# A linear recurrence inside a gemm stream: level exponentials begun two levels ahead, key transposes later in two heads

## The chip, the cores and the metric

The kernel runs on one core of one Trainium2 chip. The metric is the device time of one execution in microseconds (us). Five engines work side by side: TensorE (PE in the profile; its weight loads are PEld), VectorE (DVE), ScalarE (ACT), GpSimd (POOL) and SyncE (SP), which here issues the loads of the weights. Each engine takes its instructions in a fixed order, and waits at an instruction until what that needs is there.

## The reference, cut to what matters

One layer of a hybrid network for 256 latent tokens and 256 context tokens, model width 2048. A joint input projection feeds two mixers: a differential attention, and a gated linear recurrence with 8 heads of 128 x 128, run in both directions. Their results are projected, gated, added and projected again; a gated MLP with a convolution follows. The change is in the recurrence:

```python
def rec_gate(f_raw, lower):
    f = lower + (1.0 - lower) * jax.nn.sigmoid(f_raw.astype(jnp.float32))
    return to_rec_heads(1.0 - f), to_rec_heads(jnp.log(f))

    def step(state, inp):
        kc, vc, gc = inp[0], inp[1], inp[2]
        b = jnp.cumsum(gc, axis=2)
        b_end = b[:, :, -1:, :]
        new_state = (jnp.exp(b_end)[:, :, 0, :, None] * state
                     + jnp.einsum('bhsk,bhsv->bhkv', kc * jnp.exp(b_end - b), vc))
        ...
        rel = jnp.exp(jnp.where(mask, b[:, :, :, None, :] - b[:, :, None, :, :], -jnp.inf))
        scores = jnp.einsum('bhtk,bhtsk,bhsk->bhts', qc, rel, kc)
        out = (jnp.einsum('bhts,bhsv->bhtv', scores, vc)
               + jnp.einsum('bhtk,bhkv->bhtv', qc * jnp.exp(b), state))
```

The score of token t for token s is a product over 128 features of q_t, k_s and the exponential of the difference of two running sums of log gates.

## The kernel before

**Gemms.** Weights come as f32 blocks of 128 x 1024 (`stage`, L65): a load into `raw`, a cast on ACT into `whi` (L72), the rest on DVE into `wlo` (L73). A projection tile takes two such blocks, called units here. A tile over latent and context tokens takes three matmuls for each 128 rows (L77 to L79, `acc<-h,whi` and `acc<-h,wlo`, 24 in a unit); one over latent tokens alone takes two (L136, L137, 16 in a unit). In the recurrence stage each head h needs four tiles: the two gates RFF and RFB and the values RI, of three matmuls, and the queries RQ, of two. The last RG tiles, of the output's gate, close the stage.

**Gates of a head.** After RFF, RFB and RQ the raw values lie in `fq`. `fold` brings RQ out of PSUM (L152 on ACT, L153 on DVE), then come a copy (L669), the sigmoid (L670), the query's product (L671), the scaling with the lower bound (L674), two lines on POOL that give k (`kkq`, L676, and `kc`, L677), two clampings (L678, L679), Ln (L680), a sum (L681), and five scans, the running sums: three into `PL` (L683), two into `PC` (L685). `PL` and `PC` have two buffers each, used in turn by the heads.

**A head's products.** `head` (L558 on) is a generator that puts down the rest of a head, and is interrupted by `yield n`. It computes `KQ` (exponentials of `PC` and `PL`, L561 to L564, and a product on DVE, L565, and on POOL, L568), transposes the values (`tp`, L597) and the scaled keys (`ktp`, L604), forms `dc` (L610 to L613: level 7 and the diagonal) and the states (`stp`, L620). The scores between the two halves of blocks of 2, 4, 8 ... 128 tokens are the levels 0 to 6. For each a factor tile `E` is made by `level(li)`: two subtractions (L586, L587), one exponential on ACT (L588), two products (L590, L591). The subtractions of levels 3 and 5 and the products of levels 2 and 4 are on POOL, all others on DVE. Four matmuls (`lv`, L629) multiply E's halves into PSUM, and DVE copies the result under a mask into the scores (`S4`, L632). At the end stands the output `op` (L637 to L640).

**What sets the order.** `tick(n)` is called after each unit of a gemm, with 2 for a three-matmul unit and 1 for another, and lets the first head in the list go on once its yields have run down; one head is served at a time, and the next one after it. So the yields set where in the gemm stream PE meets a head's products. A scheduler then orders the instructions of each engine by what depends on what and by a high priority for `stage`. `lv` has three PSUM buffers, the tag `ar` of the factors 16, `whi` and `wlo` three, `raw` four.

Of the kernel before, what the change touches and what calls it, by code (L numbers as in the profile page):

```python
# [41 lines left out]
def body(ctx, tc, cst_d, sel_d, cb_d, ccol_d, wn_d, xT_d, xc_d, lam_d, rope_d, mask_d, wm_d, wg0_d, win_d, wba_d,  # L42
# [325 lines left out]
    with ExitStack() as esa:  # L368
# [19 lines left out]
        with ExitStack() as es:  # L388
# [100 lines left out]
            for h in range(8):  # L489
                bg_rate[0] = BG_ATT0 if h < 2 else BG_ATT  # L490
                ks = in_tile(AK + h)
                kf = at.tile([P, 512], F32, tag="kf", name="kf")
                act.copy(kf[:, 256:], ks[:, 256:])
                kr = at.tile([P, T], F32, tag="qkr", name="kr", bufs=2)
                act.copy(kr, ks[:, :256])
                rope_apply(kf[:, :256], kr)
                kT = at.tile([P, 2, 512], F32R, tag="kT", name="kT", bufs=2)
                act.copy(kT[:, 0], kf)
                dve.tensor_sub(kT[:, 1], kf, kT[:, 0].bitcast(F32))

                vs = in_tile(AV + h)
                if AV + h in g0raw:
                    vr = vs
                else:
                    vr = big.tile([P, 512], F32, tag="ar", name="vr", bufs=16)
                    act.copy(vr, vs)

                qs = in_tile(AQ + h)
                qr = at.tile([P, T], F32, tag="qkr", name="qr", bufs=2)
                fold(qr, qs)  # L510
                rope_apply(qr, qr)
                qT = at.tile([P, 2, T], F32R, tag="qT", name="qT", bufs=2)
                act.copy(qT[:, 0], qr)
                dve.tensor_sub(qT[:, 1], qr, qT[:, 0].bitcast(F32))
                start(head(h, kT, vr, qT))
# [11 lines left out]
        with ExitStack() as es:  # L527
# [29 lines left out]
            def head(h, kkq, kc, PL, PC, vr):  # L557
# [16 lines left out]
                def level(li):  # L574
                    c = LEVELS[li]
                    shp = [P, 2, T // (2 * c), c]
                    Lv = AL.rearrange("p (d n w c) -> p d n w c", d=2, w=2, c=c)[:, :, :, 0]
                    Rv = AR.rearrange("p d (n w c) -> p d n w c", w=2, c=c)[:, :, :, 1]
                    rl = PL[:, 1:3, 0:T].rearrange("p d (n w) -> p d n w", w=2 * c)[:, :, :, c:c + 1].broadcast_to(shp)
                    rr = PL[:, 0:2, 0:T].rearrange("p d (n w) -> p d n w", w=2 * c)[:, :, :, c:c + 1].broadcast_to(shp)  # L580
                    E = big.tile([P, 2, T], F32, tag="ar", name="E", bufs=16)
                    Ev = E.rearrange("p d (n w c) -> p d n w c", w=2, c=c)
                    Lm = kkq[:, 0::2].rearrange("p d (n w c) -> p d n w c", w=2, c=c)[:, :, :, 0]
                    Rm = kkq[:, 1:3].rearrange("p d (n w c) -> p d n w c", w=2, c=c)[:, :, :, 1]
                    eng = pool if li in (3, 5) else dve
                    eng.tensor_tensor(Ev[:, :, :, 0], rl, Lv, ALU.subtract)  # L586
                    eng.tensor_tensor(Ev[:, :, :, 1], Rv, rr, ALU.subtract)  # L587
                    act.activation(E, E, AF.Exp)  # L588
                    eng = pool if li in (2, 4) else dve
                    eng.tensor_tensor(Ev[:, :, :, 0], Ev[:, :, :, 0], Lm, ALU.mult)  # L590
                    eng.tensor_tensor(Ev[:, :, :, 1], Ev[:, :, :, 1], Rm, ALU.mult)  # L591
                    return E

# [4 lines left out]
                vn = rt.tile([P, 4, P], F32, tag="vn", name="vn", bufs=2)  # L598
                act.copy(vn, tp)
                E7 = level(7)  # L600
                yield 2 if h in (0, 1, 7) else 1
                kt_ = rps.tile([P, 4, P], F32, tag="aux", name="ktp", bufs=2)
                for i in range(4):
                    pe.transpose(kt_[:, i], KQ[:, 0, i // 2, (i % 2) * P:(i % 2 + 1) * P], ident)  # L604
                kn = big.tile([P, 4, P], F32, tag="ar", name="kn", bufs=16)
                act.copy(kn, kt_)
                E = level(0)
                yield 1
                dc = rps.tile([P, 4, P], F32, tag="aux", name="dc", bufs=2)
                pe.matmul(dc[:, 1], E7[:, 0, 0:P], E7[:, 1, P:], start=True, stop=True)  # L610
# [10 lines left out]
                stn = rt.tile([P, 2, P], F32, tag="stn", name="stn", bufs=2)  # L621
                act.copy(stn, sp[:, 0:2])

                for li in range(7):
                    En = level(li + 1) if li < 6 else None
                    yield 1
                    lvp = rps.tile([P, 2, P], F32, tag="lv", name="lv", bufs=3)
                    for m in range(2):
                        pe.matmul(lvp[:, m], E[:, 0, m * P:(m + 1) * P], E[:, 1, m * P:(m + 1) * P],  # L629
                                  start=True, stop=True)  # L630
                    for m in range(2):
                        dve.copy_predicated(out=S4[:, 3 * m], mask=masks[:, li].bitcast(U32), data=lvp[:, m])  # L632
                    E = En
                yield 2
                op = rps.tile([P, 4, P], F32, tag="aux", name="op", bufs=2)
                o2 = op[:, 0:2].rearrange("p a b -> p (a b)")
# [20 lines left out]
            for h in range(8):  # L657
# [31 lines left out]
                else:  # L689
                    vr = big.tile([P, 512], F32, tag="ar", name="vr", bufs=16)  # L690
                    act.copy(vr, ri)
                start(head(h, kkq, kc, PL, PC, vr))
                if h == 0:

# [318 lines left out]
```

## Time and profile before

| | |
|---|---|
| median of three runs | 1888.81 us (1885.11 to 1890.86) |
| the profiled execution's own time | 1883.4 us |
| its span | 1881.6 us |
| PE busy | 1833.5 us, 97% |
| DVE busy | 1353.2 us, 72% |
| ACT busy | 997.2 us, 53% |
| POOL busy | 382.1 us, 20% |
| mean granted clock of TensorE | 0.995 |

The span is the time from the first to the last instruction of the profiled execution. Busy times are of the whole program; the recurrence stage lies from about 410 to 810 us. The rows further down say, for each line, when an engine began, how long it worked and, in brackets, how long it stood idle before and what ended that. Matmuls overlap their neighbours, so the distance of their starts says what one takes of PE's time, not their duration.

### The profile page before, as it was taken

How to read it: one execution, taken by the hardware profiler on the slowest of the kernel's cores; microseconds unless marked ns; L12 is line 12 of the kernel's file. 1: busy time of each engine (PE TensorE's matmuls, PEld its weight loads, DVE VectorE, ACT ScalarE, POOL GpSimd, SP SyncE). 2: the span in 40 equal slices, each digit the busy share in tenths (PEclk: the TensorE clock that was granted, in tenths of full speed). 3: DMA queues.
4: the chain of work that ended last, by engine and by line, in shares of the span. 5: the costliest groups of instructions: out<-in, count | busy, mean ns of one | idle time of the engine just before them, and what ended most of it. 6: DMA issues, size and time to landing. Idle time of an engine off the chain costs nothing.

```text
span 1881.6 us, 27926 instructions
## 1 busy us (share of the span) xinstructions
PE 1833.5 (97%) x10416; PEld 1558.2 (83%) x10416; DVE 1353.2 (72%) x2131; ACT 997.2 (53%) x1507; POOL 382.1 (20%) x328
## 2 busy tenths in 40 slices
PE   7999999999999999999999999999999999999997
PEld 4777777887788888888888889888888888888886
DVE  4449989779866667988886779776777677654444
ACT  4336444557655556744455557555555555534342
POOL 0002111103223333411111111222222222211111
PEclk9999999999999999999999999999999999999998
DMA  9977777474233333688997665666656666666664
GB/s 387 369 266 256 229 230 238 142 239 137 93 113 112 102 103 122 211 302 305 321 321 249 190 191 179 192 190 190 191 190 191 190 191 190 182 194 187 193 188 132
DMA packets 108711, 385.69 MB, mean 205 GB/s; under 512 B 12320, under 2 KB 12448, under 8 KB 108576
## 3 DMA queue, kind: packets, MB, share of 16 engines
q1 hardware_dynamic: 108576, 383.92, 63.1%
q8 instruction: 81, 1.33, 0.3%
q14 instruction: 54, 0.44, 0.1%
HBM read 381.78 MB, written 2.10 MB: 204 GB/s over the span
## 4 chain that ended last, share of the span: by engine, by line
PE 78%; DVE 11%; DMA 6%; issue 3%; ACT 2%; POOL 0%; SPq 0%; DVEq 0%; ACTq 0%; POOLq 0%
PE macc L136 30%; PE macc L137 15%; PE acc L136 6%; DMA bgraw<-in_wm 5%; PE acc L77 5%; PE acc L79 5%; PE acc L78 5%; DVE wlo L73 3%; PE acc L137 3%; PE g L187 2%; DVE bgraw L93 2%; PE acc L187 2%; PE nat L187 2%; PE lv L629 1%; ACT whi L72 1%
## 5 line engine op out<-in xcount | busy, mean ns | idle before, releaser
L73 DVE TENSOR_TENSOR wlo<-raw,whi 128x1024 fp32r<-128x1024 f32 (+1 forms) x514 | 628.6, 1224 | 240.0 <-ACT whi L72 234.7
L72 ACT CAST whi<-raw 128x1024 fp32r<-128x1024 f32 (+1 forms) x514 | 530.9, 1034 | 422.1 <-PE macc L136 159.2
L136 PE MATMUL macc<-h,whi 128*128 128x512 f32 x1344 | 466.0, 391 | 0.0
L137 PE MATMUL macc<-h,wlo 128*128 128x256 f32 x1344 | 376.3, 280 | 0.0
L136 PE MATMUL acc<-h,whi 128*128 128x512 f32 x896 | 320.9, 400 | 0.0
L136 PEld LDWEIGHTS macc<-h,whi 128*128 128x128 f32 x1344 | 251.3, 187 | 55.1
L137 PEld LDWEIGHTS macc<-h,wlo 128*128 128x128 f32 x1344 | 254.0, 189 | 0.0
L137 PE MATMUL acc<-h,wlo 128*128 128x256 f32 x896 | 252.5, 282 | 1.2 <-DVE wlo L73 1.0
L136 PE MATMUL macc<-f,whi 128*128 128x512 f32 x704 | 244.1, 391 | 0.0
L77 PE MATMUL acc<-h,whi 128*128 128x512 f32 x528 | 212.1, 402 | 0.0
L79 PE MATMUL acc<-h,wlo 128*128 128x512 f32 x528 | 207.3, 393 | 0.3 <-DVE wlo L73 0.3
L78 PE MATMUL acc<-h,whi 128*128 128x512 f32 x528 | 206.4, 391 | 0.0
L136 PEld LDWEIGHTS acc<-h,whi 128*128 128x128 f32 x896 | 168.4, 188 | 37.7 <-issue 0.4
L137 PE MATMUL macc<-f,wlo 128*128 128x256 f32 x704 | 197.1, 280 | 0.0
L137 PEld LDWEIGHTS acc<-h,wlo 128*128 128x128 f32 x896 | 169.3, 189 | 4.9 <-DVE wlo L73 4.3
L93 DVE SCALAR_TENSOR_TENSOR bgraw<-bgraw,cb 128x1024 f32<-128x1024 f32 x105 | 133.0, 1268 | 36.8 <-DMA bgraw<-in_wm 36.0
L136 PEld LDWEIGHTS macc<-f,whi 128*128 128x128 f32 x704 | 131.6, 187 | 28.9
L884 POOL TENSOR_TENSOR u<-u 128x256 f32<-128x256 f32 x44 | 69.2, 1572 | 326.5 <-DVE u L879 286.5
L137 PEld LDWEIGHTS macc<-f,wlo 128*128 128x128 f32 x704 | 133.1, 189 | 0.0
L77 PEld LDWEIGHTS acc<-h,whi 128*128 128x128 f32 x528 | 99.2, 188 | 22.8 <-issue 4.3
L79 PEld LDWEIGHTS acc<-h,wlo 128*128 128x128 f32 x528 | 99.1, 188 | 22.6 <-DVE wlo L73 0.8
L78 PEld LDWEIGHTS acc<-h,whi 128*128 128x128 f32 x528 | 99.3, 188 | 19.2 <-issue 0.4
(752 smaller groups left out, 2674.4 us busy)
## 6 DMA issues: line engine op xcount, KB each, us to landing
raw<-in_win SPq DMA_DIRECT2D x178, 512.0 KB, 4.3
raw<-in_wup SPq DMA_DIRECT2D x168, 512.0 KB, 3.6
bgraw<-in_wm SPq DMA_DIRECT2D x105, 512.0 KB, 4.7
raw<-in_wdn SPq DMA_DIRECT2D x80, 512.0 KB, 3.6
nraw<-in_wn SPq DMA_DIRECT2D x64, 512.0 KB, 7.5
raw<-in_wout SPq DMA_DIRECT2D x32, 512.0 KB, 3.5
raw<-in_wm SPq DMA_DIRECT2D x23, 512.0 KB, 3.6
raw<-in_wba SPq DMA_DIRECT2D x16, 512.0 KB, 4.7
```

The lines of the kernel that those rows point to most:

```text
L72: act.copy(hi[:, :n], raw[:, :n])
L73: dve.tensor_sub(lo[:, :n], raw[:, :n], hi[:, :n].bitcast(F32))
L77: pe.matmul(ps, wh, xh, start=first, stop=False)
L78: pe.matmul(ps, wh, xl, start=False, stop=False)
L79: pe.matmul(ps, wl, xh, start=False, stop=last)
L93: dve.scalar_tensor_tensor(raw, raw, 1.0, c_, op0=ALU.mult, op1=ALU.mult, accum_out=dst)
L136: pe.matmul(ps, hi[:, c_], xs[k][:, :, :T], start=k == 0, stop=False)
L137: pe.matmul(ps[:, :T], lo[:, c_], xs[k][:, 0, :T], start=False, stop=k == len(xs) - 1)
L187: tc.keep_in_program_order(pe.matmul(*args, **kw))
L629: pe.matmul(lvp[:, m], E[:, 0, m * P:(m + 1) * P], E[:, 1, m * P:(m + 1) * P], start=True, stop=True)
L884: pool.tensor_tensor(cs[1], cs[0], cs[1], ALU.mult)
```

## The change

Two things in `head`. The yield ahead of the key transposes is 3 for head 0 and 4 for head 1, where it was 2 for both; head 7 keeps 2 and the others 1. And the factors are kept in a list: `level(1)` is put down ahead of the loop and `level(li + 2)` in it, where before it was `level(li + 1)`.

```diff
-                yield 2 if h in (0, 1, 7) else 1
+                yield {0: 3, 1: 4, 7: 2}.get(h, 1)
                 kt_ = rps.tile([P, 4, P], F32, tag="aux", name="ktp", bufs=2)
                 for i in range(4):
                     pe.transpose(kt_[:, i], KQ[:, 0, i // 2, (i % 2) * P:(i % 2 + 1) * P], ident)
                 kn = big.tile([P, 4, P], F32, tag="ar", name="kn", bufs=16)
                 act.copy(kn, kt_)
-                E = level(0)
+                Es = [level(0)]
                 yield 1
...
+                Es.append(level(1))
                 for li in range(7):
-                    En = level(li + 1) if li < 6 else None
+                    if li < 5:
+                        Es.append(level(li + 2))
                     yield 1
+                    E = Es.pop(0)
                     lvp = rps.tile([P, 2, P], F32, tag="lv", name="lv", bufs=3)
...
-                    E = En
                 yield 2
```

Two lines more, so line numbers from L629 on are higher by 2 or 3 after the change (lv L632, its copies L635, op L639 to L642, the sum behind Ln L683, the scans L685 and L687).

In the rows that follow, `ktp`, `dc`, `acc`, `op`, `lv`, `E`, `kkq` and the others are the tiles named above, and the number behind a name tells its buffers apart; a bracket says on which engines the instruction waits. On PE at head 1's key transposes, in the kernel before:

```order
L79 MATMUL acc_4188<-h15_1185,wlo_4244 128x512
L604 MATMUL ktp_4271<-ident_68,KQ_4219 128x128 [waits DVE_49]
L604 MATMUL ktp_4271<-ident_68,KQ_4219 128x128
L604 MATMUL ktp_4271<-ident_68,KQ_4219 128x128 [waits Activation_49]
L604 MATMUL ktp_4271<-ident_68,KQ_4219 128x128
L610 MATMUL dc_4284<-E_4235 128x128 [waits DVE_49,PE_49,Activation_49]
L611 MATMUL dc_4284<-E_4235 128x128
L613 MATMUL dc_4284<-kkq_4013,ksum_4225 128x128 [waits Pool_49]
```

and after the change:

```order
L77 MATMUL acc_4336<-h7_668,whi_4339 128x512
L78 MATMUL acc_4336<-h7_668,whi_4339 128x512
L79 MATMUL acc_4336<-h7_668,wlo_4340 128x512
L604 MATMUL ktp_4369<-ident_68,KQ_4249 128x128 x4
L610 MATMUL dc_4382<-E_4265 128x128 [waits Activation_49]
L611 MATMUL dc_4382<-E_4265 128x128
L613 MATMUL dc_4382<-kkq_4008,ksum_4255 128x128 [waits Pool_49]
```

They moved back by 56 matmuls of the gemms, into the middle of a later tile, and wait for nothing that is not waited for before.

On PE at the end of head 1, where its output is formed, in the kernel before:

```order
L79 MATMUL acc_4492<-h15_1185,wlo_4536 128x512
L637 MATMUL op_4563<-KQ_4219,stn_4320 128x256 [waits PE_49]
L638 MATMUL op_4563<-KQ_4219,stn_4320 128x256
L639 MATMUL op_4563<-S4_4289,vn_4233 128x256 [waits DVE_49]
L640 MATMUL op_4563<-S4_4289,vn_4233 128x256 [waits DVE_49]
L77 MATMUL acc_4573<-h0_219,whi_4576 128x512 [waits Activation_49]
```

and after the change:

```order
L79 MATMUL acc_4554<-h15_1185,wlo_4599 128x512
L639 MATMUL op_4628<-KQ_4249,stn_4424 128x256 [waits PE_49]
L640 MATMUL op_4628<-KQ_4249,stn_4424 128x256
L641 MATMUL op_4628<-S4_4387,vn_4263 128x256 [waits DVE_49]
L642 MATMUL op_4628<-S4_4387,vn_4263 128x256 [waits DVE_49]
L136 MATMUL acc_4638<-h0_219,whi_4641 128x512 [waits Activation_49]
```

Before, a three-matmul tile followed on head 1's output, with head 2's transposes in its middle, and the RQ tile came only then; now the RQ tile of head 3 (L136) follows at once, and head 2's transposes come behind it.

On DVE where head 3's gates are finished (from the sum behind Ln on), in the kernel before:

```order
L681 TENSOR_TENSOR fq_4491<-fq_4491 128x1024 [waits Activation_49]
L73 TENSOR_TENSOR wlo_4965<-raw_4962,whi_4964 128x1024 [waits DMAHW5_49,Activation_49]
L683 SCALAR_TENSOR_TENSOR PL1_3625<-ones_73,fq_4491 128x256 [waits DVE_49]
L683 SCALAR_TENSOR_TENSOR PL1_3625<-ones_73,fq_4491 128x256 x2
L685 SCALAR_TENSOR_TENSOR PC1_3627<-ones_73,fq_4491 128x256 x2
L632 COPY_PREDICATED S4_4677<-masks_3608,lv_4861 128x128
L632 COPY_PREDICATED S4_4677<-masks_3608,lv_4872 128x128 [waits PE_49]
```

and after the change:

```order
L590 TENSOR_TENSOR E_4781<-E_4781,kkq_4099 128x128x2 [waits Activation_49]
L591 TENSOR_TENSOR E_4781<-E_4781,kkq_4099 128x128x2
L683 TENSOR_TENSOR fq_4453<-fq_4453 128x1024 [waits Activation_49]
L590 TENSOR_TENSOR E_4828<-E_4828,kkq_4099 128x32x8 [waits Activation_49]
L685 SCALAR_TENSOR_TENSOR PL1_3625<-ones_73,fq_4453 128x256 [waits DVE_49]
L685 SCALAR_TENSOR_TENSOR PL1_3625<-ones_73,fq_4453 128x256
L73 TENSOR_TENSOR wlo_4951<-raw_4948,whi_4950 128x1024 [waits DMAHW5_49,PE_49,Activation_49]
L685 SCALAR_TENSOR_TENSOR PL1_3625<-ones_73,fq_4453 128x256
L687 SCALAR_TENSOR_TENSOR PC1_3627<-ones_73,fq_4453 128x256 x2
L635 COPY_PREDICATED S4_4772<-masks_3608,lv_4823 128x128 [waits PE_49]
L635 COPY_PREDICATED S4_4772<-masks_3608,lv_4823 128x128
L591 TENSOR_TENSOR E_4828<-E_4828,kkq_4099 128x32x8
```

Before, all factors of head 2 are made some 20 rows ahead of this piece, and only copies of late levels (lv_4861 is level 4) stand here; now level 1's and level 3's factors (E_4781 and E_4828) stand among the gates' lines, and the copy of level 0 (lv_4823) behind the scans.

## Rows read from the trace of the kernel before

**Rows 1.** The page's first part: busy time, share, instructions of each engine.

```profile
PE 1833.5 (97%) x10416; PEld 1558.2 (83%) x10416; DVE 1353.2 (72%) x2131; ACT 997.2 (53%) x1507; POOL 382.1 (20%) x328
```

**Rows 2.** Waits of PE, 410 to 810: releaser, us in total, times, longest.

```profile
PE ktp L604 <- DVE KQ L565: 2.8, 1, 2.8
PE lv L629 <- ACT E L588: 1.7, 1, 1.7
PE op L639 <- DVE S L632: 1.4, 1, 1.4
PE lv L629 <- DVE E L591: 1.0, 2, 0.6
...
PE op L640 <- DVE S L632: 0.3, 1, 0.3
```

**Rows 3.** Stretch table, heads 2 to 6: busy by engine, clock, DMA share, GB/s.

```profile
520.00:788.00 268.00, 268.00 (x1437) 230.74 (x1436) 196.61 (x373) 162.42 (x227) 94.20 (x89) 1.00 0.39 121
```

**Rows 4.** Timeline of PE at head 1's start: start, us, instruction, idle before.

```profile
479.08 0.39 PE L79 MATMUL acc<-h,wlo 128*128 128x512 f32 x1
482.27 1.11 PE L604 MATMUL ktp<-ident,KQ 128*128 128x128 f32 x4 [2.80 <-DVE KQ L565]
...
484.92 0.77 PE L136 MATMUL acc<-h,whi 128*128 128x512 f32 x1
```

**Rows 5.** Timeline of PE, the same work of a later head.

```profile
616.04 0.60 PE L597 MATMUL tp<-ident,vr 128*128 128x128 f32 x4
616.48 0.60 PE L604 MATMUL ktp<-ident,KQ 128*128 128x128 f32 x4
622.37 0.38 PE L610 MATMUL dc<-E 128*128 128x128 f32 x2
...
623.26 1.06 PE L620 MATMUL stp<-vn,kn 128*128 128x128 f32 x8
```

**Rows 6.** Stretch table around two waits; the granted clock stands behind POOL.

```profile
455.00:460.00 5.00, 3.01 (x16) 2.39 (x17) 5.00 (x11) 4.98 (x10) 3.42 (x4) 1.00 0.22 66
480.00:485.00 5.00, 2.73 (x13) 2.52 (x13) 4.90 (x10) 3.54 (x6) 1.33 (x2) 0.72 0.00 0
```

**Rows 7.** Timeline of all engines: the gates of head 4, from RQ's end.

```profile
584.29 0.61 PE L629 MATMUL lv<-E 128*128 128x128 f32 x4
...
589.11 1.28 ACT L670 ACTIVATE fq<-fq 128x1280 f32<-128x1280 f32 x1
...
591.91 2.06 POOL L676 TENSOR_SCALAR kkq<-fq 128x512 f32<-128x512 f32 x1 [9.25 <-DVE fq L674]
...
596.65 1.92 ACT L680 ACTIVATE fq<-fq 128x2048 f32<-128x2048 f32 x1
...
599.74 1.22 DVE L73 TENSOR_TENSOR wlo<-raw,whi 128x1024 fp32r<-128x1024 f32 x1
600.88 1.84 DVE L683 TENSOR_TENSOR_SCAN PL<-ones,fq 128x256 f32<-128x256 f32 x3
602.65 1.25 DVE L685 TENSOR_TENSOR_SCAN PC<-ones,fq 128x256 f32<-128x256 f32 x2
603.81 0.47 DVE L632 COPY_PREDICATED S<-masks,lv 128x128 f32<-128x128 uint32 x2
603.96 1.28 ACT L588 ACT_TABLE_LOAD   x1
605.25 0.63 ACT L588 ACTIVATE E<-E 128x512 f32<-128x512 f32 x1
```

**Rows 8.** Timeline of PE: two levels, then half a three-matmul tile, then two levels.

```profile
590.23 1.05 PE L629 MATMUL lv<-E 128*128 128x128 f32 x8
...
596.57 1.05 PE L629 MATMUL lv<-E 128*128 128x128 f32 x8
```

**Rows 9.** Timeline of DVE and POOL at head 1's last scans.

```profile
477.86 2.29 DVE L685 TENSOR_TENSOR_SCAN PC<-ones,fq 128x256 f32<-128x256 f32 x2
...
477.88 1.72 POOL L568 TENSOR_TENSOR KQ<-KQ,kkq 128x512 f32<-128x512 f32 x1 [2.79 <-ACT KQ L563]
```

## The prediction, made before the changed kernel had run

> **What bounds the kernel now.** I read the page's busy line first: TensorE (PE) is busy for 1833.5 us of a span of 1881.6 us [rows 1], so an edit pays only where it takes away idle time of PE, and it costs wherever it makes PE wait. Then I asked what PE waits for in the recurrence stage, 410 to 810 us [rows 2]. There is little to gain: the transposes of the scaled keys (ktp) once for 2.8 us, level products (lv) three times for 2.7 together, and the products of the output (op) for 1.4 and 0.3. The stretch table says where none of this lies: from 520 to 788 us PE is busy for 268.00 of 268.00 us [rows 3]. Heads 2 to 6 have not one visible stall. The four waits lie in heads 0 and 1 and at the tail.
>
> The profiled execution took 1883.4 us, the median of the three timed runs is 1888.81. The sum is made against 1883.4, and 5.4 is added at the end.
>
> **What the change removes.** Head 1's key transposes begin at 482.27 after an idle of 2.80, while the gemm in front ended by 479.5 [rows 4]; they wait for KQ, which VectorE (DVE) has ready only then. In the new order they stand 56 matmuls further back; at the pace of a three-pass unit (below, 5.46 us for 24) that is about 12.7 us, so KQ is long there. Gain 2.80. The wait also costs clock: the granted clock is 0.72 in 480 to 485 [rows 6], between the levels of 2.4 and 1.2 GHz, and PE did nothing in the 2.8 us before. From the first ktp to the first gemm behind head 1's dc, 2.65 us pass [rows 4]; a later head has 0.44 for four transposes and 0.89 for dc [rows 5], 1.33. That is 1.32 lost, and about 0.35 more in the slow gemms behind: 1.67. A wait of 1.69 in 455 to 460 left the clock at 1.00 [rows 6], so only the long one costs it. Two crumbs: op in head 0 is reached 24 gemms later, which ends its 0.3 wait, and at the tail three products come back to back, which I put at 0.6 less than the 1.8 lost there now (bounds -2 to +1). Gains: 2.80 + 1.67 + 0.3 + 0.6 = **5.4 us**. Head 0's stalls for E stay: the order of DVE and ScalarE (ACT) there is nearly the same.
>
> **What it moves.** The yields act in heads 0 and 1 alone, but the flows run one behind the other, so the delay is never made good: from head 1 on, all of a head's work stands three ticks later. In the order before, a head's key transposes stand two halves of a three-pass tile ahead of the next head's RQ unit, and all its level factors E are made on DVE ahead of that unit. After it, op of the old head stands directly in front of RQ, the key transposes directly behind, and the factors fall into the time in which DVE and ACT build the next head's gates. That chain is already long. In head 4 it starts at the end of RQ (PE 584.29), the sigmoid runs at 589.11, POOL's part at 591.91, Ln 596.65 to 598.57, the five scans from 600.88 to 602.65 + 1.25 = 603.90 [rows 7]: **19.6 us** from RQ to the last scan. It costs nothing now because PE has its factors already.
>
> What PE will do in that time, by its own durations: ktp 0.44, half a tile, dc and states, half a tile, two levels, half a tile, level 2, then level 3. Two levels and half a tile took 596.57 - 590.23 = 6.34 [rows 8]; a level is four matmuls as ktp is, 0.44 [rows 5]; so half a tile is 6.34 - 0.88 = 5.46, and dc with the states, 16 such matmuls, 1.77. Sum: 0.44 + 5.46 + 1.77 + 5.46 + 6.34 + 0.44 = **19.9 us**. At that point PE needs two things: level 3's factor, and a free PSUM buffer, since lv has three and level 0's must have been copied out. In the new order both instructions stand behind the scans on DVE.
>
> So for head 2, from RQ's end: Ln ends at 14.3; its table reload and one exponential, 1.28 + 0.63 [rows 7], bring 16.2; the first factor half 16.6; two scans of 0.6, 17.8; the split wlo of 1.2, whose cast ends then, 19.0; third scan 19.6; two scans in 1.2, 20.8; two copies of 0.2, 21.2; the second half 21.5. PE was ready at 19.9: a stall of **1.6** with nothing in the way. POOL, though, multiplies level 4's factor from 16.9 on. Two PC scans beside POOL at work took 2.29 [rows 9], beside an idle POOL 1.25 [rows 7]; that, and a slower wlo, makes 3.1.
>
> The Trainium skill has a rule for this. "GPSIMD Engine Reference", section 1 (Specifications), says that GpSimd's SBUF interfaces are shared with VectorE, in contention with DVE instructions with two SBUF inputs. The two scan rows agree; by the rule alone the 3.1 would stand, since each scan reads two operands. Another rule speaks for less: "ScalarE: Activation LUTs", section Table sets, says that one set holds both exp and ln. By that no reload would follow Ln and a stall would be up to 0.7 shorter. The trace has the reload, 1.28 at 603.96, so the measurement decides.
>
> By the same walk, each with its order: heads 5 and 6 are as head 2 (1.6 to 3.1 each). Head 3 has its wlo ahead of all scans and the factor behind the copies: 3.1 to 4.4. Head 4 has the factor already, and only the copies gate: 1.2 to 2.2. In head 1 the key transposes lie in a gates unit; level 0's exponential stands behind the sigmoid on ACT, and level 1's factor halves stand before and behind the scans: 3.4 to 4.8 for the two. Sum: 12.5 without contention, 20.7 with. I take 14.6, nearer the low end, since POOL's products cover only part of the scans and a PC pair beside it alone explains 1 us of the 3.
>
> **The two-ahead exponentials** add no instruction; they ask for E earlier, and the pool of 16 buffers gives room. Between bounds of 0 and -2.7 (all the lv waits of [rows 2]) I take 0: those waits are in head 0, whose order hardly moves.
>
> **Forecast.** 1883.4 - 5.4 + 14.6 = 1892.6 in the frame of the profiled run, **1898** on the median. Own range with 12.5 and 20.7: 1896 to 1904, and a tail error of 2 to each side gives 1894 to 1906.
>
> **The rivals.**
> Rival A, the gate chain gets shorter. Now the sigmoid starts 4.8 us behind RQ's end, 589.11 - 584.29 [rows 7], and lv copies and a wlo stand between. If the new order starts it 1.7 us earlier, the 1.6 of heads 2, 5 and 6 and most of head 4's go; heads 1 and 3 keep 4 to 6. Against it: the kn copy and a level's exponential take the same place on ACT. About as before: 1889.
> Rival B, the factors are covered. It ends on the faster side. The mechanism is a single slack, level 3's place 19.9 us behind RQ; if the scans are done 1.6 to 3 us sooner than my walk, in all heads, no stall is left, and the time is 1888.8 - 5.4 = 1883.5. It decides where wlo and scans swap or the exponential needs no reload. For it: the stall is the small difference of two sums of 20. Against: six heads, each with an own order, all late in the walk.
> Rival C, stalls feed the clock. Head 1's wait of 2.8 cost 1.67 in clock. If heads 1 and 3 pass 2.8 and contention is full, 20.7 + 2 x 1.67 - 5.4 gives +18.6: 1907.
> Rival D, the yields do nothing behind head 1 because the program's order is set otherwise; the new order rules that out, as RQ stands directly behind op in all later heads.
>
> **How the numbers follow.** A measurement here can tell about 0.3% (5.7 us) from no change. Forecast 0.52, rival A 0.23, rival B 0.15, rival C 0.10. Faster by over 5.7 us, under 1883.1, is about two thirds of B: 0.10. Slower by over 5.7, above 1894.5: the forecast less its low edge, and C: 0.57. The same: 0.33. To leave out no more than 2 in 10 the range must reach from B's upper part, 1884, to C's, 1907.
>
> **What would show it.** The wait row of ktp for KQ gone, and 480 to 495 at clock 1.00, confirm the gains. For each of heads 1 to 6 a wait of 1 to 5 us at lv, put down to DVE's copies or the last factor half, confirms the cost; the stretch 520 to 788 should show 10 to 17 us of idle PE where it has none. If it shows none, rival B is right. The walk fails at its start if the sigmoid begins less than 4 us behind RQ, and at its end if the scans are done before 19.9. A first stall at level 0, or at ktp, would mean that the late place itself, not the copies, is the cost.

## The result: 27 us slower, and where they are

The changed kernel took 1915.94 us in the median of five runs (1912.59 to 1917.78), against 1888.81: a ratio of 1.0146, interval 1.0132 to 1.0160: 27.1 us by the medians, 27.6 by the ratio. The sign was forecast; the time lies 18 us above the forecast and 9 above the range. The profiled execution of after took 1912.59 us, its span is 1910.8.

The page's first part, busy times of after, answers to [rows 1]:

```profile
PE 1843.8 (96%) x10416; PEld 1568.8 (82%) x10416; DVE 1359.1 (71%) x2131; ACT 1007.6 (53%) x1515; POOL 382.0 (20%) x328
```

PE runs the same 10416 matmuls and is busy 10 us longer: some of them were slower. ACT has eight instructions more, 10.4 us of work; these are table loads of 1.28 us, seven of them ahead of the level exponentials (L588).

The waits of PE in the recurrence stage and the tail, 405 to 850 us of after (releaser, us in total, times, longest), answer to [rows 2]:

```profile
PE lv L632 <- DVE E L591: 22.3, 9, 4.3
PE lv L632 <- DVE S L635: 2.9, 2, 1.7
PE lv L632 <- ACT E L588: 1.7, 1, 1.7
PE ktp L604 <- issue: 0.8, 1, 0.8
PE acc L79 <- DVE wlo L73: 0.3, 1, 0.3
```

The wait of 2.8 for KQ is gone, as it should be. In its place PE waits 22.3 us for the second half of level factors (L591) and 2.9 for copies (L635). In all 28.0 us, where the stage of before had 8.6.

The single waits, from the timeline of PE (start, us, instruction, idle before); the first two are head 1, then heads 2, 3, 4, 5, 6, and the last two belong to the tail, head 7:

```profile
503.62 0.68 PE L632 MATMUL lv<-E 128*128 128x128 f32 x4 [3.13 <-DVE E L591]
512.14 2.04 PE L632 MATMUL lv<-E 128*128 128x128 f32 x8 [2.58 <-DVE E L591]
564.96 1.19 PE L632 MATMUL lv<-E 128*128 128x128 f32 x4 [3.91 <-DVE E L591]
617.89 1.15 PE L632 MATMUL lv<-E 128*128 128x128 f32 x4 [4.33 <-DVE E L591]
667.36 0.68 PE L632 MATMUL lv<-E 128*128 128x128 f32 x4 [1.72 <-DVE S L635]
716.96 1.19 PE L632 MATMUL lv<-E 128*128 128x128 f32 x4 [3.48 <-DVE E L591]
768.16 1.19 PE L632 MATMUL lv<-E 128*128 128x128 f32 x4 [3.34 <-DVE E L591]
810.73 0.68 PE L632 MATMUL lv<-E 128*128 128x128 f32 x4 [0.55 <-DVE E L591]
821.60 0.68 PE L632 MATMUL lv<-E 128*128 128x128 f32 x4 [1.16 <-DVE S L635]
```

Heads 1 to 6: 22.5 us. The four matmuls behind the waits of heads 2, 3, 5 and 6 take 1.15 us and more, where those behind head 1's first wait and behind those of heads 4 and 7 take 0.68: that is the clock. The stretch table (busy time by engine, then granted clock, DMA share, GB/s) shows it, first for the heads that answer to [rows 3], then around head 2's wait:

```profile
520.00:800.00 280.00, 263.18 (x1348) 225.23 (x1347) 187.05 (x341) 155.80 (x212) 85.51 (x82) 0.97 0.35 105
560.00:572.00 12.00, 8.09 (x29) 6.61 (x28) 10.50 (x24) 2.82 (x4) 2.98 (x3) 0.72 0.29 88
```

PE is idle for 16.8 us of a stretch of heads that had no idle time at all. Read in steps of 2 us, the time lost to a clock under 2.4 GHz (2 us times one minus the granted clock, summed over 410 to 850) is 10.24 us, where it was 1.72 before: 1.70 behind head 1's second wait, 3.42 behind head 2's, 1.72, 1.70 and 1.70 behind those of heads 3, 5 and 6. Idle time +19.4 and clock +8.5 make 27.9, which is the difference of the runs. (The two profiled executions differ by 29 us. Ahead of 410 us, where the code is the same, the one of after is 2.6 us later; by the same sum the clock cost 6.8 us there, and 3.4 before.)

### The profile page after: what moved, and what is told of

It is laid out like the page before. It is cut to its first block, busy times and chain, and to the rows that moved or that the text cites. A ratio compares the mean times of both kernels' runs of the same rounds, so it can differ in the third digit from the quotient of the medians.

```text
span 1910.8 us, 27963 instructions
## 1 busy us (share of the span) xinstructions
PE 1843.8 (96%) x10416; PEld 1568.8 (82%) x10416; DVE 1359.1 (71%) x2131; ACT 1007.6 (53%) x1515; POOL 382.0 (20%) x328
## 4 chain that ended last, share of the span: by engine, by line
PE 73%; DVE 12%; DMA 6%; issue 4%; ACT 4%; POOL 1%; SPq 0%; DVEq 0%; ACTq 0%; POOLq 0%
PE macc L136 29%; PE macc L137 15%; PE acc L136 6%; DMA bgraw<-in_wm 5%; DVE wlo L73 4%; PE acc L77 3%; PE acc L78 3%; PE acc L79 3%; PE acc L137 3%; PE g L187 2%; PE acc L187 2%; PE nat L187 2%; DVE bgraw L93 2%; ACT whi L72 1%; PE lv L632 1%
## 5 line engine op out<-in xcount | busy, mean ns | idle before, releaser
L136 PE MATMUL macc<-h,whi 128*128 128x512 f32 x1344 | 466.0, 391 | 0.0
L136 PE MATMUL acc<-h,whi 128*128 128x512 f32 x896 | 323.7, 403 | 0.0
L136 PEld LDWEIGHTS macc<-h,whi 128*128 128x128 f32 x1344 | 251.5, 187 | 54.8
L136 PE MATMUL macc<-f,whi 128*128 128x512 f32 x704 | 244.1, 391 | 0.0
L77 PE MATMUL acc<-h,whi 128*128 128x512 f32 x528 | 215.5, 408 | 0.0
L78 PE MATMUL acc<-h,whi 128*128 128x512 f32 x528 | 209.5, 397 | 0.0
L136 PEld LDWEIGHTS acc<-h,whi 128*128 128x128 f32 x896 | 169.5, 189 | 38.2 <-issue 0.5
L136 PEld LDWEIGHTS macc<-f,whi 128*128 128x128 f32 x704 | 131.7, 187 | 28.7
L77 PEld LDWEIGHTS acc<-h,whi 128*128 128x128 f32 x528 | 101.8, 193 | 23.6 <-issue 4.3
L78 PEld LDWEIGHTS acc<-h,whi 128*128 128x128 f32 x528 | 101.7, 193 | 19.5 <-issue 0.4
```

The source lines that it names most:

```text
L77: pe.matmul(ps, wh, xh, start=first, stop=False)
L78: pe.matmul(ps, wh, xl, start=False, stop=False)
L136: pe.matmul(ps, hi[:, c_], xs[k][:, :, :T], start=k == 0, stop=False)
```

## Inside one wait: head 2

The end of RQ is the start of the next matmuls of PE, the key transposes at 540.63; the next head's sigmoid starts at 546.36, and Ln (on ACT) runs from 553.91 to 555.82:

```profile
540.63 0.60 PE L604 MATMUL ktp<-ident,KQ 128*128 128x128 f32 x4
546.36 1.27 ACT L672 ACTIVATE fq<-fq 128x1280 f32<-128x1280 f32 x1
553.91 1.91 ACT L682 ACTIVATE fq<-fq 128x2048 f32<-128x2048 f32 x1
```

Then DVE, from its timeline in after:

```profile
555.86 1.23 DVE L683 TENSOR_TENSOR fq<-fq 128x1024 f32<-128x1024 f32 x1 [1.56 <-ACT fq L682]
557.80 0.43 DVE L590 TENSOR_TENSOR E<-E,kkq 128x256 f32<-128x256 f32 x1 [0.72 <-ACT E L588]
558.14 1.77 DVE L685 TENSOR_TENSOR_SCAN PL<-ones,fq 128x256 f32<-128x256 f32 x2
559.84 1.70 DVE L73 TENSOR_TENSOR wlo<-raw,whi 128x1024 fp32r<-128x1024 f32 x1
561.47 1.10 DVE L685 TENSOR_TENSOR_SCAN PL<-ones,fq 128x256 f32<-128x256 f32 x1
562.49 1.61 DVE L687 TENSOR_TENSOR_SCAN PC<-ones,fq 128x256 f32<-128x256 f32 x2
564.03 0.46 DVE L635 COPY_PREDICATED S<-masks,lv 128x128 f32<-128x128 uint32 x2
564.41 0.41 DVE L591 TENSOR_TENSOR E<-E,kkq 128x256 f32<-128x256 f32 x1
```

and POOL in the same time:

```profile
558.37 1.00 POOL L590 TENSOR_TENSOR E<-E,kkq 128x256 f32<-128x256 f32 x1 [4.36 <-ACT E L588]
559.34 1.13 POOL L591 TENSOR_TENSOR E<-E,kkq 128x256 f32<-128x256 f32 x1
560.42 1.60 POOL L586 TENSOR_TENSOR E<-PL 128x256 f32<-128x256 f32 x1
561.99 0.99 POOL L587 TENSOR_TENSOR E<-PL 128x256 f32<-128x256 f32 x1
```

The factor's first half is done at 558.2; its second stands behind five scans, a wlo and two copies, and is done at 564.8. Beside POOL, the first two scans took 1.77 instead of 1.2, wlo 1.70 instead of 1.22, the third scan 1.10 instead of 0.6, the PC pair 1.61 instead of 1.25. Against the walk, counted from RQ's end:

| | walk | trace |
|---|---|---|
| Ln ends | 14.3 | 15.2 |
| first half of level 3's factor | 16.6 | 17.6 |
| two scans | 17.8 | 19.3 |
| wlo | 19.0 | 20.9 |
| third scan | 19.6 | 21.9 |
| PC pair | 20.8 | 23.5 |
| second half | 21.5 | 24.2 |
| PE wants it | 19.9 | 20.4 |
| wait | 1.6 | 3.9 |

The order of events is the forecast one, line by line; 0.9 us were lost ahead of Ln, where the sigmoid starts 5.7 us behind RQ and not 4.8 (beside heads 5 and 6 Ln ends at 14.5, as in the walk). The rest goes with POOL's work beside the scans, as a later run shows; this ended with level 5's subtractions and not, as in the walk, with level 4's products. Since PE too came 0.5 later than in the walk, 2.3 of the 2.7 us are left in the wait.

## Which half of the change does it

Theory L: the later yields put every head's factors among the next head's gates, and the loss follows from that place. Rival A of these runs (not the prediction's): beginning two levels ahead pulls exponentials and half factors in between Ln and the scans. The change was taken apart. The kernel before was timed again beside each group of runs (medians 1891.67, 1888.66 and 1891.33 us), and the ratios are against those times.

**Only the yields.**

```diff
-                yield 2 if h in (0, 1, 7) else 1
+                yield {0: 3, 1: 4, 7: 2}.get(h, 1)
```

> Only the later yields of heads 0 and 1 (3 and 4 for 2 and 2) are taken over; the level exponentials are begun one level ahead, as before the change. Theory L (the late place of the heads in the gemm stream puts the level factors among the next head's gates): most of the loss stays, 1908 to 1920 us, with waits of 1.5 to 5 us of PE at the level products in heads 1 to 6 and some 10 us of clock. Rival A (beginning two levels ahead pulls exponentials and half factors in between Ln and the scans, and that is the loss): 1884 to 1892, no such waits.

Measured: 1915.28 us, ratio 1.0118 (1.0085 to 1.0151). Its waits:

```profile
PE lv L629 <- DVE E L591: 18.5, 9, 3.4
PE lv L629 <- POOL E L591: 2.0, 1, 2.0
PE lv L629 <- DVE S L632: 1.7, 1, 1.7
```

and 8.58 us of clock lost by the same sum.

**Only the two-ahead exponentials**: the rest of the change, with the yields of before.

> Only the two-ahead exponentials are taken over; the yields are those of before. Theory L: no difference that can be measured, 1886 to 1892, PE idle 0 between 520 and 788 us, the 2.8 us wait of the key transposes for KQ still there. Rival A: 1905 or more, with waits at the level products in the later heads.

Measured: 1891.59 us, ratio 1.0000 (0.9985 to 1.0014), and no wait from 520 to 790 us. The wait that was to go is there:

```profile
PE ktp L604 <- DVE KQ L565: 2.4, 1, 2.4
```

Rival A is out: without the late yields the two-ahead exponentials cost nothing that can be measured, and with the late yields alone most of the loss is there. Whether they add something beside the late yields stays open. The trace of the yields alone has 3.0 us less idle time and 1.7 less clock loss than that of after, and its ratio, 1.0118, is lower than 1.0146, but the two intervals overlap.

## How late is too late

**Two ticks.** Against the changed kernel:

```diff
-                yield {0: 3, 1: 4, 7: 2}.get(h, 1)
+                yield {0: 2, 1: 4, 7: 2}.get(h, 1)
```

> The changed kernel with the yield of head 0 back at 2; head 1 keeps 4, so all later heads stand two ticks late instead of three. In its order the factors of heads 2 to 6 come ahead of the next head's gates again. Theory L with a threshold at the third tick: the waits at the level products of heads 2 to 6 are gone, the wait for KQ (2.8) and its clock loss (1.7) too: 1883 to 1890, faster than before by up to 5 us. If the loss grows with each tick: two thirds of 27, about 1907.

Measured: 1913.57 us, ratio 1.0123 (1.0106 to 1.0141). Both expectations missed: there is no gain at two ticks, and the loss isn't two thirds either. The order had told truly that the factors come early; I had overlooked the copies. Its waits:

```profile
PE lv L632 <- DVE S L635: 17.9, 9, 4.2
PE lv L632 <- DVE E L591: 2.7, 3, 1.7
```

Now it is PSUM. Level 2's product is copied half ahead of the scans and half behind them, and level 5 waits for that buffer, in head 3 (timelines of PE, then DVE):

```profile
613.83 0.87 PE L632 MATMUL lv<-E 128*128 128x128 f32 x4 [2.06 <-DVE S L635]
```

```profile
609.34 1.22 DVE L73 TENSOR_TENSOR wlo<-raw,whi 128x1024 fp32r<-128x1024 f32 x1
610.48 1.85 DVE L685 TENSOR_TENSOR_SCAN PL<-ones,fq 128x256 f32<-128x256 f32 x3
612.24 1.25 DVE L687 TENSOR_TENSOR_SCAN PC<-ones,fq 128x256 f32<-128x256 f32 x2
613.41 0.67 DVE L635 COPY_PREDICATED S<-masks,lv 128x128 f32<-128x128 uint32 x3
```

In heads 2 and 4 the waits behind the copies are these:

```profile
555.75 0.88 PE L632 MATMUL lv<-E 128*128 128x128 f32 x4 [1.88 <-DVE S L635]
657.11 0.71 PE L632 MATMUL lv<-E 128*128 128x128 f32 x4 [1.91 <-DVE S L635]
```

So a head that stands later by two ticks meets the same scans with another of its steps.

**Ticks given back.** The same, and head 1's last yield as well:

```diff
-                yield 2
+                yield 0 if h == 1 else 2
                 op = rps.tile([P, 4, P], F32, tag="aux", name="op", bufs=2)
```

> As the run with two ticks in head 1, but head 1 gives its ticks back: its yield of 2 ahead of the output product becomes 0, so heads 2 to 7 stand as before the change. Theory L: heads 2 to 6 without a wait, the wait for KQ gone with its clock loss, against it a wait of 1 to 2 us at head 1's output product, which follows its last level at once: 1884 to 1888. Rival A: 1905 or more, as the two-ahead exponentials stay.

Measured: 1893.44 us, ratio 1.0017 (1.0004 to 1.0030). Heads 2 to 6 have no wait, though head 1's key transposes are late and the exponentials two ahead; the wait for KQ is gone. The forecast size failed: head 1 waits 4.3 us at a level instead, which eats what was won, clock included (1.72 lost, as before).

```profile
PE lv L632 <- DVE S L635: 4.3, 1, 4.3
```

With this the place of heads 2 to 7 is shown to carry the loss: this run differs from the one with two ticks in head 1's last yield alone, and with heads 2 to 7 at the old place the loss of some 23 us falls to some 3.

## What makes the place dear

Theory Q: PE waits because copy and second half stand behind the scans in DVE's queue, not because the work is late as such. Rival: the exponential with its reload, or POOL, ends last anyway.

**Copies and products first**, in the changed kernel:

```diff
+                    with tc.high_priority(offset=200):
                         eng.tensor_tensor(Ev[:, :, :, 0], Ev[:, :, :, 0], Lm, ALU.mult)
                         eng.tensor_tensor(Ev[:, :, :, 1], Ev[:, :, :, 1], Rm, ALU.mult)
...
+                    with tc.high_priority(offset=200):
                         for m in range(2):
                             dve.copy_predicated(out=S4[:, 3 * m], mask=masks[:, li].bitcast(U32), data=lvp[:, m])
```

> The changed kernel, late yields and all, but the two masked copies of a level and the two products of its factor get a higher priority, so that on DVE they stand ahead of the scans and of the wlo behind them; nothing else is touched. Theory Q (PE waits because copy and factor stand behind the scans in DVE's queue, not because the work is late as such): by the walk level 3's factor is done some 18 us behind RQ, PE wants it at 20.4, so the waits of heads 2 to 6 go and with them their clock loss; head 1 may keep 3 to 5 us: 1886 to 1896. Rival (the exponential and its table reload on ACT, or POOL, end last): waits of 2 us and more stay in most heads, 1905 or more.

Measured: 1902.23 us, ratio 1.0070 (1.0056 to 1.0083). Half of the loss is gone, 13.7 of 27; less than expected. Its waits:

```profile
PE lv L633 <- DVE E L592: 7.9, 4, 5.2
PE lv L633 <- DVE S L637: 5.1, 4, 2.0
PE acc L137 <- DVE wlo L73: 2.5, 3, 1.6
```

In heads 2 to 6 level waits of 1.0, 2.0, 0, 0.6 and 0 are left of 16.8, and no clock is lost behind them. Head 1 keeps 5.2 with 3.42 of clock, the tail waits 3.2 (1.8 before), and new is that gemms wait for wlo, 2.5: the scans and wlo now stand behind the factors. For heads 2 to 6 Q holds; the price moved in part.

**Copies first**: the second of the two edits alone.

> As the run with copies and products first, but only the copies get the priority; the second half of level 3's factor stays behind the scans. If the free PSUM buffer is what ends last: 1890 to 1898. If the factor is (the wait rows name L591): the wait of head 4, put down to the copies, goes (1.7), the others stay, 1908 to 1918.

Measured: 1919.72 us, ratio 1.0163 (1.0148 to 1.0178), no better than the change itself, 1.0146; the intervals overlap. Head 4's wait for the copy is gone and no row names the copies any more; heads 1, 2, 5 and 6 wait longer for the factor, and 15.3 us of clock are lost instead of 10.2:

```profile
PE lv L632 <- DVE E L591: 25.7, 7, 6.0
```

So at three ticks the factor's second half ends last, not the free buffer.

**The same priority at two ticks**, copies alone, where the copies were named:

> The kernel with two ticks in head 1, and the copies of the levels with the higher priority. There the factors were ready and the wait rows named the copies, L635. Theory Q: the waits of heads 2 to 6 go, head 1's 4.2 at least in part: 1884 to 1891. Rival (the copies are late because PE itself reaches the levels late): 1905 or more.

Measured: 1894.46 us, ratio 1.0033 (1.0018 to 1.0047), against 1.0123 without it: heads 2 to 6 keep not one wait of a microsecond. The 1884 to 1891 were missed because KQ comes later. On DVE head 0's copies now stand ahead of head 1's gates, and a wlo ahead of KQ's product; KQ is done 36.7 us behind head 0's key transposes instead of 33.5, so that the wait for it came back (3.7 us, with 1.70 of clock). At the tail op waits 2.8.

**POOL's share.** Theory C: POOL's products beside the scans are what made the waits longer than the walk's low end.

```diff
-                    eng = pool if li in (2, 4) else dve
+                    eng = pool if li == 2 else dve
```

> The changed kernel with the products of level 4 on DVE instead of POOL; on DVE they come behind the scans and the copies, so POOL no longer multiplies while DVE scans. Theory C (POOL beside the scans is what made the waits longer than the walk without it): in head 2 the wlo falls from 1.70 to 1.2, the third scan from 1.10 to 0.6, the PC pair from 1.61 to 1.25, and its wait from 3.9 to 2.0 to 2.8; in all 1 to 1.5 us less in heads 2, 3, 5 and 6, and where a wait gets short enough its clock loss of 1.7 goes too: 1902 to 1911. Rival (the scans are slowed by ACT or by something else): wait and time as they were, 1913 to 1918.

Measured: 1905.94 us, ratio 1.0092 (1.0076 to 1.0107), 10 us less. DVE in head 2, in the same order as above but for two products behind the last row:

```profile
556.82 1.27 DVE L685 TENSOR_TENSOR_SCAN PL<-ones,fq 128x256 f32<-128x256 f32 x2
558.00 1.20 DVE L73 TENSOR_TENSOR wlo<-raw,whi 128x1024 fp32r<-128x1024 f32 x1
559.12 0.69 DVE L685 TENSOR_TENSOR_SCAN PL<-ones,fq 128x256 f32<-128x256 f32 x1
559.72 1.25 DVE L687 TENSOR_TENSOR_SCAN PC<-ones,fq 128x256 f32<-128x256 f32 x2
560.88 0.47 DVE L635 COPY_PREDICATED S<-masks,lv 128x128 f32<-128x128 uint32 x2
561.26 0.42 DVE L591 TENSOR_TENSOR E<-E,kkq 128x256 f32<-128x256 f32 x1
```

and PE's wait:

```profile
561.83 1.19 PE L632 MATMUL lv<-E 128*128 128x128 f32 x4 [2.12 <-DVE E L591]
```

POOL is idle meanwhile: level 5's subtractions, which no longer queue behind level 4's products there, are done by 554. The first two scans are back at 1.27, wlo at 1.20, the third scan at 0.69, the PC pair at 1.25; these four together give 1.77 us, and the wait of head 2 fell by 1.79, from 3.91 to 2.12. Heads 1 to 6 together wait 14.9 us instead of 22.5, and 6.84 us of clock are lost instead of 10.24; 1.72 of that is new, behind a wait of 2.84 in head 7. Theory C is shown, and its size was a little low: heads 2, 3, 5 and 6 won 1.2 to 1.8 us each. Of the 22.5 us 7.6 went with level 4's products off POOL, and 14.9 stay.

## Looking for a version that beats both

Three more runs looked for the 4.5 us that head 1's wait for KQ costs in the kernel before, 2.80 of idle time and 1.72 of clock. Copies and products first, on two ticks:

> Two ticks in head 1 (head 0 back at 2), and copies and factor products of the levels with the higher priority. Theory Q: no waits in heads 2 to 6; what is left is head 1 (0 to 4 us with 1.7 of clock) and the tail (1 to 3): 1883 to 1893. If the priority costs the gates (wlo or Ln come late), waits for wlo of 1 to 3 us show and it is 1893 or more.

Measured 1890.64 us, ratio 1.0005 (0.9992 to 1.0019). On the kernel that gives the ticks back:

> Head 1's ticks given back, and copies and products with the higher priority. In the run with the ticks given back head 1 kept one wait of 4.3 us for a copy and 1.7 of clock. Theory Q: that wait falls to 0 to 2 us and the clock stays: 1883 to 1889, the only candidate here that may beat the kernel before. Rival: the copy waits for PE's own late levels, 1889 to 1894.

Measured 1888.54 us, ratio 0.9997 (0.9981 to 1.0012). And on the kernel before, with nothing else:

> The kernel before with nothing but the higher priority for copies and products. Theory Q: it has no waits in heads 2 to 6 that this could take away, so within 0.3%: 1884 to 1894; a gain of up to 4.5 us only if the wait for KQ in head 1 goes too.

Measured 1890.98 us, ratio 1.0000 (0.9988 to 1.0012). None differs measurably from the kernel before. In the middle one no clock is lost in the stage, and the wait for KQ is 1.7; in return head 1 waits 1.3 at a level, a gemm 1.1 (0.4 before), and op 1.9 (1.7 before). In the last one the wait for KQ grew to 3.8. Two ticks and the priority show that a place two ticks late is harmless where DVE serves PE first; at three ticks, with the same priority, 13 us of loss stayed. What head 1 loses could not be won, and nothing faster was found.

## Why the prediction missed the size

**What bounds, and the gains: right.** No slack in heads 2 to 6. The wait for KQ and its clock loss went: from 480 to 510 the granted clock is 1.00 in after, and the loss of before there was 1.72 (forecast 1.67):

```profile
480.00:510.00 30.00, 26.43 (x137) 21.94 (x135) 22.87 (x37) 21.34 (x28) 8.38 (x8) 1.00 0.36 116
```

The tail was put at 0.6 less; 0.55 + 1.16 is 1.71 against 1.8, so nothing was won. (Rival B's 1888.8 - 5.4 is 1883.4 and not 1883.5; nothing hangs on it.)

**The two-ahead exponentials at 0: right** by the run with them alone; beside the late yields their share is open, as said.

**The mechanism: right.** The waits stand at the levels, in all heads 1 to 6, put down to the second factor half, in head 4 to the copies, as named, and the stretch of heads 2 to 6 has 16.8 us of idle time, where 10 to 17 was the sign. The prediction's rivals A and B (a shorter chain, all covered) fell: in the gates beside heads 2 to 6 the sigmoid starts 5.0 to 5.7 us behind RQ's end and Ln ends 14.5 to 16.0 behind it; in the kernel before, in the same heads' gates, it was 4.5 to 5.0 and 14.0 to 14.5.

**The sum of new waits: the step that failed first.** Between 12.5 and 20.7 the prediction took 14.6 because POOL's products covered only part of the scans. Measured 22.5, above both ends:

| head | bounds | measured | with level 4 on DVE |
|---|---|---|---|
| 1 | 3.4 to 4.8 | 5.71 | 4.74 |
| 2 | 1.6 to 3.1 | 3.91 | 2.12 |
| 3 | 3.1 to 4.4 | 4.33 | 3.14 |
| 4 | 1.2 to 2.2 | 1.72 | 1.68 |
| 5 | 1.6 to 3.1 | 3.48 | 1.67 |
| 6 | 1.6 to 3.1 | 3.34 | 1.52 |

In the last column heads 2 to 6 lie within 0.6 of the low bounds, so the walk itself was sound there (head 2's 0.5 is the late Ln, less PE's own delay); contention was the normal case and its price too small. The forecast took 2.1 us of it for all six heads and had put it at 1.5 in head 2 at full price, from a pair of scans and a slower wlo; it measured 1.8 there, as all five scans and the wlo were slowed. The Trainium skill ("GPSIMD Engine Reference", section 1, Specifications) names just this contention with two-input DVE instructions; the runs bear it out, with wlo at 1.70 beside POOL and 1.20 without it.

**The clock: the step that failed next.** The forecast charged new waits with no clock at all. Rival C had this mechanism, with 1.67 for each of two heads; it too came out short, at 1907. From one wait of 1.69 without a loss and one of 2.80 with one, I had drawn that only waits near 2.8 pay. Measured: 10.24 us behind five of the nine waits listed above, among them one of 2.58; head 1's first wait of 3.13 paid nothing, head 2's 3.91 paid 3.42. With two ticks in head 1, waits of 1.88 and 1.91 us brought one. A length from which it is paid can't be read from these rows.

The forecast was short by 7.9 us of waits and 10.2 of clock, together its error of 18. With measured waits and clock the sum of the prediction comes out: 22.5 + 10.2 - 2.80 - 1.72 - 0.3 is 27.9, measured 27.6.

## What to carry to other kernels

A late start ahead of a serial chain need not stay local when the flows run one behind the other; here it reached every later head. Follow the shifted work to the place it takes in the next period, and see what else the same queues do there. Where PE has no slack, charge each new wait with the clock behind it, and price an instruction beside a busy GpSimd at its slower row as the normal case. Before a step is moved for the sake of one wait, put the work that PE waits for ahead in its engine's queue, and see whether the move is still harmful.

## What had not been expected of the hardware

- Losses of clock came in two sizes. Over all runs' recurrence stages a wait cost nothing, 1.70 to 1.72, or 3.40 to 3.42 us, and its length alone doesn't tell which: 3.13 cost nothing, 4.33 cost 1.72, 3.91 cost 3.42.
- In head 1 DVE stood still for 4.25 us at a multiplication of the background stream, whose weights had not landed, while the sigmoid, whose result the query product takes, had ended at 492.7. The query product stands behind that multiplication on DVE and began at 496.23. In the kernel before the wait at this place was 1.40 us. In the chain of the prediction it had no place. What of head 1's 5.71 it makes was not tried:

```profile
493.94 1.23 DVE L93 SCALAR_TENSOR_TENSOR raw<-raw,cb 128x1024 f32<-128x1024 f32 x1 [4.25 <-DMA raw<-in_wm]
```

- A table load of 1.28 us stands between Ln and the next exponential in the trace, and with the factors among the gates another one between the sigmoid and Ln (in head 2 at 549.07). The Trainium skill ("ScalarE: Activation LUTs", section Table sets) says that one set holds both exp and ln, by which the load behind Ln would not be needed; the trace of this kernel has it, behind head 2's Ln at 555.84 as behind head 4's before [rows 7]. The load between the sigmoid and Ln did not lengthen the chain: beside heads 3, 5 and 6 Ln ends 14.5 us behind RQ's end, against 14.3 to 14.5 in the kernel before.
